# Layer 0's first projection slice by slice, its norm held back, and padded tiles in a two-layer hybrid encoder on one NeuronCore

## The chip, the cores and the metric

The kernel runs on one core of a Trainium2 chip. The core has five engines that run side by side and wait for each other through semaphores: TensorE (PE in the profile, with its weight loads as PEld), VectorE (DVE), ScalarE (ACT), GpSimd (POOL) and SyncE (SP), which here only issues the transfers (DMA) from HBM into SBUF. Matrix products land in PSUM, which has eight banks of 512 float32 columns. The metric is the time of one execution in microseconds on the device, less is better.

## What is computed

A trunk of two layers over 512 tokens of width 1024. Each layer projects the normalised input into queries, keys and values of two groups of heads, runs windowed attention with a sink logit (group A) and differential attention (group B), projects back, and then runs a gated feed-forward part with a depthwise convolution of width 3. Cut to what matters:

```python
for l in range(DEPTH):                                  # 2
    h = rmsnorm(x, g_attn[l])                           # 512 x 1024
    qa, ka, va, qb, kb, vb = split(h @ w_in[l])         # 2304 columns
    qa, ka, qb, kb = (rope(rmsnorm(t, gain)) for t in (qa, ka, qb, kb))
    ya = windowed_gqa_sink(qa, ka, va, sink[l])         # 8 q heads, 2 kv heads
    yb = rmsnorm(diff_attention(qb, kb, vb, lam), subln[l]) * (1 - lambda_init)
    x = x + concat(ya, yb) @ w_out[l]
    h = rmsnorm(x, g_ffn[l])
    gate, val = split(h @ w_up[l])                      # 2 x 2816 columns
    x = x + (silu(conv3(gate)) * val) @ w_down[l]
```

All is float32. The kernel makes each product out of three TensorE products of split operands: high times high, high times low, low times high, where "high" is the value rounded to TensorE's fp32r format and "low" is what the rounding left.

## The kernel before

**Products.** `mm3` (L197) issues the three products of one 128-row slice of the contraction: L198 (high, high), L199 (high, low) and L200 (low, high). The 1024 rows of `x` lie in SBUF as eight tiles `x0` to `x7` of 128 rows by 512 tokens, so a projection is a sum over k = 0..7. In the input projections the stationary operand is a 128-token piece of the normalised input and the moving one a 256-column piece of the weights; in the up-projection (`up`), the down-projection (`dn`) and the first parts of the output projection (`wo`) the weights are stationary and the activations are moving, 512 columns wide.

**Weights.** The weights come as a fixed list of units of at most 512 KB. `emit_unit` (L176) issues one transfer into a tile `wr` (2 buffers), rounds it on ACT into `wh` (L185) and takes the low part on DVE, or on POOL for a part of the units, into `wl` (L186); `wh` and `wl` have 3 buffers each. The first two units, which hold the group A key and value columns of layer 0 (`akv`), are split in four pieces each. `next_unit` keeps three units ahead.

**The norm.** The norm's scale is not put on the input but on the projection's result. `Norm.add` (L212) makes the high part (`na_h`, ACT L216) and the low part (`na_l`, DVE L217) of x times its gain; `Norm.square` squares and sums: in layer 0 the squares of `x0` to `x3` and their sum are made on POOL (L226, L231), those of `x4` to `x7` on ACT (L228) with sums on DVE. `Norm.rms` (L233) sums over the partitions by TensorE products with a column of ones (`na_ss`, L237), and DVE (L240) and POOL (`na_r`, L248, a power of -0.5) turn them into `r_tok`, one factor for each token. Only what reads a projection's bank needs `r_tok`: `scaled` (L330) on ACT.

**The first stage of layer 0.** SP issues `cols`, `x0`, unit 0, `x1` to `x4`, unit 1, `x5` to `x7`, and then the small tables. The projection of `akv` needs two PSUM banks of two 256-column halves, then `aq0` and `aq1` (group A queries, four head columns each) follow; `qk_out` (L336) turns each bank into rotated, normalised and transposed queries or keys, with much of its work on POOL: a power (L248), a product with the rotation table (L362) and a sum (L363). The rest of layer 0's projections are woven with the attention by a planner (`weave`, L125). The order in which instructions stand on each engine is then settled by the scheduler of the tile framework at build time, so it isn't simply the order of the code.

**Places in SBUF.** Tiles are laid out one pool tag behind the other in each partition. As built, the tiles of the tags `wh`, `wl` and `hid0`/`hid1` (the high and low parts of normalised inputs: `na_h`, `na_l`, `nf_h`, `nf_l`) start at bytes 46,144, 58,432, 76,864 and 93,248, multiples of 64. What comes after the tile `rows` (520 numbers, 2,080 bytes) starts 32 bytes above a multiple of 64: `keep` from 129,376, `pair` from 179,168, `prob` from 211,936. `keep` and `pair` hold `act` (the feed-forward's activations, moving operand of `dn`), `yh`/`yl` (moving in `wo`), queries, keys and values; `prob` holds the transposed probabilities (moving in `pv_a` and `yb`). The tag `tmp` has 2,056 bytes and so alternates between the two kinds of start.

Of the kernel before, what the change touches and what calls it, by code (L numbers as in the profile page):

```python
# [16 lines left out]
P = 128  # L17
# [19 lines left out]
FIRST_SQ = 4  # L37
# [5 lines left out]
def kernel(  # L43
# [35 lines left out]
    def tmp(name, n=S):  # L79
        return sb.tile([P, n], F32, tag="tmp", bufs=8, name=name)  # L80
# [61 lines left out]
    cols = const.tile([P, DEPTH, N_COL], F32, name="cols")  # L142
    rope_sb = const.tile([P, 2, NT, HD], F32, name="rope_sb")
    mask_sb = const.tile([P, 3 * P], F32, name="mask_sb")
    ones = const.tile([P, 1], F32, name="ones")
    nhalf = const.tile([P, 1], F32, name="nhalf")
    nc.gpsimd.memset(ones, 1.0)
    nc.gpsimd.memset(nhalf, -0.5)

# [26 lines left out]
    def emit_unit():  # L176
# [7 lines left out]
        for o in ([slice(0, k)] if i > 1 else [slice(j, j + 1) for j in range(k)]):  # L184
            nc.scalar.copy(hi[:, o], raw[:, o])  # L185
            eng.tensor_tensor(out=lo[:, o], in0=raw[:, o], in1=hi[:, o], op=ALU.subtract)  # L186
        ready.append((hi, lo))
        state["emitted"] += 1

# [13 lines left out]
    class Norm:  # L203
        def __init__(self, l, base, name):
            self.l, self.base, self.name = l, base, name
            self.first = l == 0 and base == 0
            self.x = []
            self.hi = [None] * NK
            self.lo = [None] * NK
            self.part = [sb.tile([P, S], F32, tag="tab", bufs=3, name=f"{name}_sum")]  # L210
# [10 lines left out]
        def square(self, k):  # L221
            if self.first and k == FIRST_SQ:
                self.part.append(tmp(f"{self.name}_sum2"))
            sq = self.part[-1] if k == 0 or self.first and k == FIRST_SQ else tmp(f"{self.name}_q{k}")
            if self.first and k < FIRST_SQ:
                nc.gpsimd.tensor_tensor(out=sq, in0=self.x[k], in1=self.x[k], op=ALU.mult)  # L226
            else:
                nc.scalar.activation(sq, self.x[k], AF.Square)  # L228
            if sq is not self.part[-1]:
                eng = nc.vector if self.first and k >= FIRST_SQ else nc.gpsimd  # L230
                eng.tensor_tensor(out=self.part[-1], in0=self.part[-1], in1=sq, op=ALU.add)  # L231

        def rms(self):  # L233
            acc = accum(f"{self.name}_ss")
            for t in range(NT):
                for k, sq in enumerate(self.part):
                    nc.tensor.matmul(acc[:, t:t + 1], lhsT=sq[:, t * P:(t + 1) * P], rhs=ones,  # L237
                                     start=k == 0, stop=k == len(self.part) - 1)
# [11 lines left out]
    def split_out(hi, lo, src):  # L250
        nc.scalar.copy(hi, src)
        nc.vector.tensor_tensor(out=lo, in0=src, in1=hi, op=ALU.subtract)

    warm = const.tile([P, 1], F32, name="warm")
    nc.scalar.activation(warm, ones, AF.Copy, scale=ones)
    nc.sync.dma_start(cols, col_par)
    nc.sync.dma_start(x_sb[0], x_v[:, 0])
    emit_unit()
    for k in range(1, NK):
        nc.sync.dma_start(x_sb[k], x_v[:, k])  # L260
        if k == 4:
            emit_unit()
    nc.sync.dma_start(ident, ident_in)
    nc.sync.dma_start(rope_sb, rope)
    nc.sync.dma_start(mask_sb, mask)
    norm = Norm(0, 0, "na0")
    for k in range(NK):
        norm.add(k, x_sb[k])
# [3 lines left out]
    for l in range(depth):  # L272
        lam_init = 0.8 - 0.6 * math.exp(-0.3 * l)

        rows = sb.tile([P, N_ROW], F32, tag="rows", bufs=1, name=f"rows{l}")
# [33 lines left out]
        r_tok = norm.rms()  # L309
        if l == 0:  # L310
            make_tabs((2, 3))
# [4 lines left out]
        def project(name, done, alloc):  # L316
            w = [next_unit(), next_unit()]
            for tp in range(NT // 2):
                bank = alloc(f"pj{l}_{name}_{tp}").rearrange("p (t c) -> p t c", t=2)
                for i in range(2):  # L320
                    t = 2 * tp + i
                    for k in range(NK):
                        mm3(bank[:, i], (h_in.hi[k][:, t * P:(t + 1) * P], h_in.lo[k][:, t * P:(t + 1) * P]),
# [6 lines left out]
        def scaled(name, bank, tp):  # L330
            raw = rp(name)
            for i in range(2):
                nc.scalar.activation(raw[:, i], bank[:, i], AF.Copy, scale=r_tok[:, 2 * tp + i:2 * tp + i + 1])
# [478 lines left out]
```

## Time and profile before

| | |
|---|---|
| time, median of 3 runs | 1294.73 us (1293.69 to 1295.14) |
| time of the profiled execution | 1294.65 us |
| its span in the profile | 1292.9 us, 17,021 instructions |
| mean granted TensorE clock | 0.977 |
| DVE busy | 754.8 us (58%) |
| ACT busy | 541.8 us (42%) |
| POOL busy | 359.6 us (28%) |
| HBM read, written | 99.73 MB, 2.10 MB |

The profiled execution's time is 1.75 us more than its span. In the profile a row of a timeline gives the start, the duration, the engine, the line, the operation and the names of its output and inputs; several like rows that follow each other are merged with their count. Matrix products overlap in the pipeline, so the time that one costs is the distance between the starts of two neighbours and not its duration.

### The profile page before, as it was taken

To read this page: it belongs to the slowest core of one execution; us is meant where nothing else is said; L and a number is where in the kernel's file an instruction comes from. 1 tells how busy PE (TensorE), PEld (TensorE's weight loads), DVE (VectorE), ACT (ScalarE), POOL (GpSimd) and SP (SyncE) were. 2 spreads that over 40 slices of the span, in tenths; PEclk is the share of its full clock that TensorE was granted. 3 is DMA by queue.
4 is the path that set the end of the run, shared out by engine and by line. 5 is a ranking of instruction groups with operands and counts; after the bars stand their busy time and mean duration, and the time that the engine had idled before them with its cause. 6 is when DMAs were issued, how large, how long until landed. Compare 5 with 4: busy or idle time off the path is not lost. (4 is left out here: it accounts for less than half of the span.)

```text
span 1292.9 us, 17021 instructions
## 1 busy us (share of the span) xinstructions
PE 1239.9 (96%) x6648; PEld 1040.6 (80%) x6648; DVE 754.8 (58%) x1245; ACT 541.8 (42%) x943; POOL 359.6 (28%) x354
## 2 busy tenths in 40 slices
PE   6999997989999999999999999888999999999998
PEld 6988885778888888888899889766888888888886
DVE  6678787766755334554446778756765542355532
ACT  4455564435433213333345666444443331233321
POOL 5746283114111000112247556602321110011100
PEclk8999999899999999999999999969999999999999
DMA  5312121013332333332332111201233323333232
GB/s 174 99 34 66 42 65 34 26 40 103 96 96 87 96 94 114 97 93 72 98 98 81 51 36 64 65 1 34 65 99 113 96 76 98 106 98 98 80 108 90
DMA packets 32625, 102.93 MB, mean 80 GB/s; under 512 B 3616, under 2 KB 4000, under 8 KB 32544
## 3 DMA queue, kind: packets, MB, share of 16 engines
q1 hardware_dynamic: 32544, 101.84, 25.9%
q8 instruction: 52, 0.85, 0.3%
q14 instruction: 29, 0.24, 0.1%
HBM read 99.73 MB, written 2.10 MB: 79 GB/s over the span
## 5 line engine op out<-in xcount | busy, mean ns | idle before, releaser
L185 ACT CAST wh<-wr 128x1024 fp32r<-128x1024 f32 (+3 forms) x210 | 197.5, 944 | 408.6 <-PE up L199 171.0
L199 PE MATMUL up<-nf_l,wh 128*128 128x512 f32 x704 | 274.7, 390 | 0.6 <-DVE nf_l L217 0.5
L200 PE MATMUL up<-nf_h,wl 128*128 128x512 f32 x704 | 274.1, 390 | 0.4
L198 PE MATMUL up<-nf_h,wh 128*128 128x512 f32 x704 | 273.4, 390 | 0.0
L186 DVE TENSOR_TENSOR wl<-wr,wh 128x1024 fp32r<-128x1024 f32 (+3 forms) x174 | 192.5, 1110 | 108.7 <-ACT wh L185 108.4
L718 POOL TENSOR_TENSOR cv<-cv,rb 128x512 f32<-128x512 f32 x44 | 59.2, 1346 | 519.3 <-ACT cv L717 519.3
L199 PEld LDWEIGHTS up<-nf_l,wh 128*128 128x128 f32 x704 | 132.2, 188 | 29.8 <-DVE nf_l L217 2.8
L200 PEld LDWEIGHTS up<-nf_h,wl 128*128 128x128 f32 x704 | 132.2, 188 | 28.8 <-DVE wl L186 1.5
L198 PEld LDWEIGHTS up<-nf_h,wh 128*128 128x128 f32 x704 | 132.2, 188 | 27.5 <-ACT nf_h L216 0.2
L200 PE MATMUL dn<-act,wl 128*128 128x512 f32 x352 | 139.5, 397 | 0.0
L199 PE MATMUL dn<-act,wh 128*128 128x512 f32 x352 | 139.4, 397 | 0.0
L198 PE MATMUL dn<-act,wh 128*128 128x512 f32 x352 | 138.8, 395 | 0.0
L186 POOL TENSOR_TENSOR wl<-wr,wh 128x1024 fp32r<-128x1024 f32 x36 | 86.9, 2419 | 106.4 <-ACT wh L185 106.4
L711 DVE TENSOR_TENSOR gp<-up,rb 128x512 f32<-128x512 f32 x44 | 30.3, 693 | 103.4 <-PE up L200 98.4
L199 PEld LDWEIGHTS dn<-act,wh 128*128 128x128 f32 x352 | 66.8, 190 | 16.5
L198 PEld LDWEIGHTS dn<-act,wh 128*128 128x128 f32 x352 | 66.0, 188 | 16.5
L200 PEld LDWEIGHTS dn<-act,wl 128*128 128x128 f32 x352 | 66.1, 188 | 15.5
L719 DVE TENSOR_TENSOR cv<-cv,up 128x512 f32<-128x512 f32 x44 | 30.2, 687 | 81.8 <-POOL cv L718 72.1
L522 ACT ACTIVATE e_b<-sc_b,mx_b,rqb 128x512 f32<-128x512 f32 x64 | 49.2, 773 | 49.5 <-DVE mx_b L519 45.6
L732 DVE TENSOR_TENSOR x<-x,dn 128x512 f32<-128x512 f32 x32 | 22.0, 689 | 79.7 <-PE dn L200 79.7
L717 ACT ACTIVATE cv<-cv 128x512 f32<-128x512 f32 x44 | 27.7, 631 | 71.6 <-DVE cv L716 71.5
L518 DVE TENSOR_REDUCE mx_b<-sc_b 128x2 f32<-128x1024 f32 x32 | 39.0, 1219 | 7.9 <-PE sc_b L516 7.8
(212 smaller groups left out, 2559.9 us busy)
## 6 DMA issues: line engine op xcount, KB each, us to landing
wr<-w_up SPq DMA_DIRECT2D x88, 512.0 KB, 3.6
wr<-w_in SPq DMA_DIRECT2D x36, 512.0 KB, 3.6
wr<-w_down SPq DMA_DIRECT2D x32, 384.0 KB, 3.0
wr<-w_down SPq DMA_DIRECT2D x32, 320.0 KB, 2.9
wr<-w_out SPq DMA_DIRECT2D x16, 512.0 KB, 3.6
x<-xT SPq DMA_DIRECT2D x8, 256.0 KB, 5.3
outT<-x SPq DMA_DIRECT2D x8, 256.0 KB, 2.0
rows<-row_par SPq DMA_DIRECT2D x2, 260.0 KB, 4.2
```

The costliest lines, as they stand in the source:

```text
L185: nc.scalar.copy(hi[:, o], raw[:, o])
L186: eng.tensor_tensor(out=lo[:, o], in0=raw[:, o], in1=hi[:, o], op=ALU.subtract)
L198: nc.tensor.matmul(acc, lhsT=a[0], rhs=b[0], start=start, stop=False)
L199: nc.tensor.matmul(acc, lhsT=a[0], rhs=b[1], start=False, stop=False)
L200: nc.tensor.matmul(acc, lhsT=a[1], rhs=b[0], start=False, stop=stop)
L518: nc.vector.tensor_reduce(out=mx, in_=scp, axis=AX, op=ALU.max)
L522: nc.scalar.activation(e[c], sc[c], AF.Exp, bias=mx[:, c:c + 1], scale=rq[:, c:c + 1], accum_out=lsum[:, c:c + 1])
L711: nc.vector.tensor_tensor(out=g[:, 1:S + 1], in0=acc[0], in1=rb, op=ALU.mult)
L717: nc.scalar.activation(cv, cv, AF.Silu)
L718: nc.gpsimd.tensor_tensor(out=cv, in0=cv, in1=rb, op=ALU.mult)
L719: nc.vector.tensor_tensor(out=cv, in0=cv, in1=acc[1], op=ALU.mult)
L732: nc.vector.tensor_tensor(out=x_sb[d], in0=x_sb[d], in1=acc, op=ALU.add)
```

## The change

Four things change, all but the last in the first stage of layer 0.

1. **The `akv` projection of layer 0 is run slice by slice.** The first two weight units go to tiles of their own (`first_w`, the raw part in two `prob` buffers), one 128 KB piece of weights is transferred right behind each `x_k`, and for every k the products of all four token tiles are issued into two banks (`mm`) that two products with a column of zeros (L264) have cleared.
2. **The squares are held back and leave POOL.** All eight squares are made on ACT and all seven sums on DVE. They read a scale `gate`, which DVE makes as max and min of an element of the fourth unit's split and which is always 1, so that they can't start before that split is done.
3. **The norm comes later.** One step of `aq0` is issued, then `rms`, then the work on the two `akv` banks between the steps of `aq0`. `aq1`'s first bank is taken from the score tag `sc`.
4. **Tiles are padded.** `tmp` to 528 numbers, `cols` to 112 a layer (its transfer now writes two pieces of 105 numbers to a partition), `rows` to 528; the one-column constants go into one 64-byte tile `unit`. As built, `wh`, `wl`, `hid0` and `hid1` start at 54,336, 66,624, 85,056 and 101,440, each 8,192 bytes above its old place; `keep` starts at 146,048, `pair` at 187,264 and `prob` at 37,952, and every buffer of these tags and of `tmp` starts at a multiple of 64.

```diff
-        eng = nc.gpsimd if kind in ("inb", "out") else nc.vector
-        for o in ([slice(0, k)] if i > 1 else [slice(j, j + 1) for j in range(k)]):
-            nc.scalar.copy(hi[:, o], raw[:, o])
-            eng.tensor_tensor(out=lo[:, o], in0=raw[:, o], in1=hi[:, o], op=ALU.subtract)
+        eng = nc.gpsimd if kind in ("inb", "out") else nc.vector
+        split(eng, hi, lo, raw)
...
         def square(self, k):
-            if self.first and k == FIRST_SQ:
-                self.part.append(tmp(f"{self.name}_sum2"))
...
-            if self.first and k < FIRST_SQ:
-                nc.gpsimd.tensor_tensor(out=sq, in0=self.x[k], in1=self.x[k], op=ALU.mult)
...
+            sq = self.part if k == 0 else tmp(f"{self.name}_q{k}")
+            nc.scalar.activation(sq, self.x[k], AF.Square, **({"scale": gate} if self.first else {}))
+            if k:
+                eng = nc.vector if self.first else nc.gpsimd
+                eng.tensor_tensor(out=self.part, in0=self.part, in1=sq, op=ALU.add)
...
+    for k in range(NK):
+        nc.sync.dma_start(x_sb[k], x_v[:, k])
+        nc.sync.dma_start(first_w[k // 4][0][:, k % 4], units[k // 4][0][:, k % 4])
...
+    for tp in range(2):
+        b = mm(f"pj0_akv_{tp}")
+        nc.tensor.matmul(b, lhsT=zero.broadcast_to([P, P]), rhs=zero.broadcast_to([P, S]), start=True, stop=False)
+        first_banks += [b[:, i * CW:(i + 1) * CW] for i in range(2)]
+    for k in range(NK):
+        norm.add(k, x_sb[k])
+        raw, hi, lo = (v[:, k % 4] for v in first_w[k // 4])
+        split(nc.vector, hi, lo, raw)
+        for t in range(NT):
+            mm3(first_banks[t], (norm.hi[k][:, t * P:(t + 1) * P], norm.lo[k][:, t * P:(t + 1) * P]),
+                (hi, lo), False, k == NK - 1 and t % 2 == 1)
     emit_unit()
...
+    emit_unit()
+    nc.vector.tensor_scalar(out=gate, in0=ready[-1][1][:, 0, :1], scalar1=1.0, scalar2=1.0, op0=ALU.max, op1=ALU.min)
...
-        run(proj_a(0, turn))
-        run(proj_a(1, turn))
+        if l:
+            run(proj_a(0, turn))
+        else:
+            p0 = proj_a(0, at)
+            for _ in range(FIRST_MM):
+                next(p0)
+            r_tok = norm.rms()
+            for tp in range(2):
+                akv_done(first_banks[2 * tp:2 * tp + 2], tp)
+                next(p0)
+            make_tabs((2, 3))
+            run(p0)
+        run(proj_a(1, turn if l else lambda nm: (lambda n: sc2(n)[:, 0], turn)[int(nm[-1])](nm)))
```

On PE the program now starts with the two clearing products and then takes all that needs `x0` before anything that needs `x1` (the numbers behind `na0_h` and `na0_l` are k). Before, its first rows were:

```order
L198 MATMUL pj0_akv_0_233<-wh0_85,na0_h0_119 128x256
L198 MATMUL pj0_akv_1_305<-wh0_85,na0_h0_119 128x256
L199 MATMUL pj0_akv_0_233<-wl0_86,na0_h0_119 128x256
L200 MATMUL pj0_akv_0_233<-wh0_85,na0_l0_120 128x256
L199 MATMUL pj0_akv_1_305<-wl0_86,na0_h0_119 128x256
L200 MATMUL pj0_akv_1_305<-wh0_85,na0_l0_120 128x256
L198 MATMUL pj0_akv_0_233<-wh0_85,na0_h1_123 128x256
```

Of each slice only six products stood there, those of one token tile of each bank; the products of the other two token tiles came after all eight slices, from `x0` again. Now, on PE at the same place:

```order
L264 MATMUL pj0_akv_0_106<-unit_76 128x512
L264 MATMUL pj0_akv_1_108<-unit_76 128x512
L201 MATMUL pj0_akv_0_106<-wh_f0_83,na0_h0_110 128x256
L201 MATMUL pj0_akv_1_108<-wh_f0_83,na0_h0_110 128x256
L202 MATMUL pj0_akv_0_106<-wl_f0_84,na0_h0_110 128x256
L203 MATMUL pj0_akv_0_106<-wh_f0_83,na0_l0_111 128x256
L201 MATMUL pj0_akv_0_106<-wh_f0_83,na0_h0_110 128x256
L202 MATMUL pj0_akv_0_106<-wl_f0_84,na0_h0_110 128x256
L203 MATMUL pj0_akv_0_106<-wh_f0_83,na0_l0_111 128x256
```

The rows of one slice are now twelve, and 96 for the whole projection. The column sums of the squares have moved on PE from between the two halves of `akv` to the end of `aq0`; they now stand after 94 of its 96 products, and `aq1` follows:

```order
L201 MATMUL pj0_aq0_1_470<-wh3_261,na0_h7_236 128x256
L234 MATMUL na0_ss_350<-unit_76,na0_sum_105 128x1 x4
L202 MATMUL pj0_aq0_1_470<-wl3_262,na0_h7_236 128x256
L203 MATMUL pj0_aq0_1_470<-wh3_261,na0_l7_237 128x256
L201 MATMUL pj0_aq1_0_552<-wh4_320,na0_h0_110 128x256
```

On DVE, what stood around the norm of layer 0 before was this (`na0_sum2` is the sum of `x4` to `x7`; `wl2`, `wl3` are the low parts of `aq0`'s weights, `na0_v` the mean square):

```order
L217 SCALAR_TENSOR_TENSOR na0_l7_148<-x7_71,cols_73,na0_h7_147 128x512
L296 TENSOR_SCALAR nsink0_182<-rows0_172 128x8
L300 TENSOR_TENSOR lprod0_184<-rows0_172 128x128
L231 TENSOR_TENSOR na0_sum2_161<-na0_sum2_161,na0_q7_169 128x512
L302 TENSOR_REDUCE ldot0_186<-lprod0_184 128x2
L186 TENSOR_TENSOR wl2_217<-wr2_215,wh2_216 128x1024
L306 TENSOR_SCALAR nlam0_190<-lexp0_188 128x1
L240 TENSOR_SCALAR na0_v_201<-na0_ss_192 128x4
```

Now DVE has, from the end of the slices on, the splits of two units and the gate (L275), behind an instruction that reads `rows`:

```order
L191 TENSOR_TENSOR wl2_256<-wr2_254,wh2_255 128x1024
L191 TENSOR_TENSOR wl3_262<-wr3_260,wh3_261 128x1024
L305 TENSOR_SCALAR nsink0_301<-rows0_291 128x8
L275 TENSOR_SCALAR unit_76<-wl3_262 128x1
L309 TENSOR_TENSOR lprod0_303<-rows0_291 128x128
```

Seven sums and two more splits follow there, and only then the mean square; the last rows of that piece of DVE's program are:

```order
L229 TENSOR_TENSOR na0_sum_105<-na0_sum_105,na0_q7_288 128x512
L191 TENSOR_TENSOR wl4_321<-wr4_319,wh4_320 128x1024
L315 TENSOR_SCALAR nlam0_309<-lexp0_307 128x1
L191 TENSOR_TENSOR wl5_327<-wr5_325,wh5_326 128x1024
L237 TENSOR_SCALAR na0_v_355<-na0_ss_350 128x4
```

`wl3`, `wl4` and `wl5` have moved ahead of the mean square; `wh5`, which `wl5` reads, takes the buffer of `wh2` and so waits on ACT for PE's last product with `wh2`, which is row 84 of `aq0`'s 96. Behind the attention of layer 0 the order of PE, DVE, POOL and ACT is as before.

68 lines of the change are left out of this document (31 added, 37 removed).

## The prediction

> **What bounds the kernel now.** I read the page's busy times first, then its chain, then a table of stretches, then PE's waits.
>
> ```profile
> PE 1239.9 (96%) x6648; PEld 1040.6 (80%) x6648; DVE 754.8 (58%) x1245; ACT 541.8 (42%) x943; POOL 359.6 (28%) x354
> ...
> PE 28%; DVE 0%; issue 0%
> ...
> 0.00:10.00 10.00, 2.77 (x10) 2.32 (x10) 4.62 (x6) 6.55 (x12) 4.75 (x10) 1.00 0.82 279
> 10.00:20.00 10.00, 5.60 (x25) 4.81 (x26) 10.00 (x10) 5.99 (x12) 9.83 (x10) 0.90 0.53 184
> 20.00:30.00 10.00, 10.00 (x68) 10.00 (x68) 4.88 (x11) 0.20 (x1) 1.64 (x4) 0.76 0.31 101
> ...
> 70.00:80.00 10.00, 7.69 (x50) 6.71 (x50) 9.45 (x19) 4.94 (x12) 4.75 (x2) 0.83 0.36 107
> ...
> PE pj_akv L198 <- ACT wh L185: 6.2, 1, 6.2
> PE pj_akv L200 <- DVE na_l L217: 3.8, 2, 2.1
> PE pj_akv L199 <- DVE wl L186: 1.6, 1, 1.6
> PE pt_a L470 <- DVE so_a L454: 2.2, 1, 2.2
> ```
>
> PE works 96% of the span and the chain runs through nothing else that counts, so there are two ways to a shorter time: fewer us in which PE stands or runs at a low clock, and a shorter distance between products. In the stretches (span, busy us by engine PE, PEld, DVE, ACT, POOL, then PE's clock) PE is idle for 7.2 and 4.4 us in the first two, and is granted a clock of 0.76 in the third. The last four lines are PE's waits up to 100 us: the first stage holds 11.6 of them.
>
> **Term 1: when PE gets to `aq0`.** The same projection at two clocks, and the point where `aq0` starts:
>
> ```profile
> 19.65 0.80 PE L200 MATMUL pj_akv<-wh,na_l 128*128 128x256 f32 x2 [1.70 <-DVE na_l L217]
> ...
> 24.30 0.41 PE L198 MATMUL pj_akv<-wh,na_h 128*128 128x256 f32 x1
> 24.51 0.41 PE L199 MATMUL pj_akv<-wl,na_h 128*128 128x256 f32 x1
> ...
> 24.93 0.27 PE L198 MATMUL pj_akv<-wh,na_h 128*128 128x256 f32 x1
> ...
> 31.14 0.28 PE L200 MATMUL pj_akv<-wh,na_l 128*128 128x256 f32 x1
> 31.26 0.28 PE L198 MATMUL pj_aq<-wh,na_h 128*128 128x256 f32 x1
> ```
>
> A product costs 0.21 us up to 24.9 and 0.12 us behind it: full speed comes 5.3 us after work without gaps began at 19.65. The 96 products of `akv` would take 11.5 us at full speed, yet `aq0` starts at 31.26. What feeds them, with the names' lines in ACT, DVE and SP:
>
> ```profile
> 4.53 0.72 ACT L216 ACTIVATE na_h<-x,cols 128x512 fp32r<-128x512 f32 x1 [2.20 <-DMA x<-xT]
> 5.75 1.32 ACT L185 CAST wh<-wr 128x256 fp32r<-128x256 f32 x4 [0.50 <-DMA wr<-w_in]
> 9.23 6.58 DVE L217 SCALAR_TENSOR_TENSOR na_l<-x,cols,na_h 128x512 fp32r<-128x512 f32 x4
> 20.38 0.74 DVE L217 SCALAR_TENSOR_TENSOR na_l<-x,cols,na_h 128x512 fp32r<-128x512 f32 x1
> L186 DVE TENSOR_TENSOR wl<-wr,wh x9: 418/939/1258, 6.2 to 23.4; 128x256 fp32r<-128x256 f32 x8, 128x1024 fp32r<-128x1024 f32 x1
> 11.84 3.42 POOL L231 TENSOR_TENSOR na_sum<-na_sum,na_q 128x512 f32<-128x512 f32 x2
> 2.12 1.85 SPq L260 DMA_DIRECT2D x<-xT  x4
> GB/s 0 0 0 74 194 164 377 258 311 401 336 324 365 365 377 410 434 418 369 406 406 412 378 381 381 386 402 418 336 57 0 0 0 0 0 0 0 0 0 115
> ```
>
> With POOL squaring beside it DVE needs 1.65 us for a `na_l`, and 0.74 alone; a piece of `wl` takes up to 1.26 us, and 0.42 at best. With the squares off POOL a slice costs DVE 0.74 + 0.42 = 1.16 us, ACT 0.72 + 0.33, the transfers 393 KB at about 390 GB/s (the last row, 0 to 20 us) = 1.0, and SP two issues of 0.46. DVE is the slowest: first `wl` at 4.53 + 0.72 + 1.16 = 6.4, the last at 5.25 + 8 x 1.16 = 14.5. PE needs 12 products a slice: 2.56 us at the low clock, 1.44 at the full one, so after the first slice PE is behind its data and has no gaps. If the clock opens 5.3 us later, as it did, at 11.7, 2.1 slices are done and 5.9 x 1.44 = 8.5 remain: `aq0` at 20.2. The bounds: 18.0 if the clock is open at once (6.45 + 8 x 1.44), 21.0 if it takes 7 us, a third longer than the row shows, 27 if it stays low throughout (6.45 + 20.5). The weights of `aq0` follow the slices: two units of 524 KB at 390 GB/s are 2.7 us of transfer, and the second's split ends near 18, in time.
>
> The sum of squares stood ahead of 31.26 and now stands behind; its four columns cost 0.11 each, 0.45. So **term 1 = 31.26 - 20.2 - 0.45 = 10.6 us less** (9.8 to 12.8; 3.8 with the low clock throughout).
>
> What is added here hides. The two clearing products are 512 wide in plain float32; the nearest row below has eight such products 128 wide in 1.09 us, so two take 0.9 us, 1.8 at the low clock, from about 1 to 3 while PE waits for ACT until 5.6; uncovered they would cost 2.3 us only if four times slower. `cols` in 256 pieces lands ahead of `x0`; uncovered 0.4 at most, its own transfer having taken less than 2 us. The gate is one element; the squares with a scale are at worst like `na_h`, 8 x 0.72 from about 18.4, and the sums end near 25 (27 if POOL's tables get in DVE's way), 4 us or more before PE reaches the column sums at 31.5. Behind the gate only the sums and `wl4` wait; `aq1` needs that at 32.
>
> ```profile
> 86.18 1.09 PE L470 MATMUL pt_a<-ident,so_a 128*128 128x128 f32 x8
> ```
>
> **Term 2: the norm's factor and what hangs on it.** It gets later:
>
> ```profile
> 28.48 0.16 DVE L240 TENSOR_SCALAR na_v<-na_ss 128x4 f32<-128x4 f32 x1 [3.76 <-PE na_ss L237]
> 29.90 1.03 POOL L248 TENSOR_TENSOR na_r<-na_v,nhalf 128x4 f32<-128x4 f32 x1
> 35.20 1.19 POOL L248 TENSOR_TENSOR rs_ka<-sv_ka,nhalf 128x4 f32<-128x4 f32 x1 [4.28 <-DVE sv_ka L348]
> 38.72 0.73 POOL L363 TENSOR_TENSOR raw_kv<-raw_kv,sq_ka 128x256 f32<-128x256 f32 x1
> 46.07 1.75 POOL L248 TENSOR_TENSOR rqa<-sv_qa,nhalf 128x8 f32<-128x8 f32 x1 [4.19 <-DVE sv_qa L351]
> 47.79 1.29 POOL L362 TENSOR_TENSOR raw_qa<-raw_qa,tab 128x512 f32<-128x512 f32 x1
> 70.28 4.75 POOL L186 TENSOR_TENSOR wl<-wr,wh 128x1024 fp32r<-128x1024 f32 x2 [2.44 <-ACT wh L185]
> 70.52 5.18 DVE L454 TENSOR_SCALAR so_a<-so_a,rl_a 128x256 f32<-128x256 f32 x4
> ```
>
> Before, it was there at 30.9. Now the mean square waits on DVE behind `wl5`: its buffer is free after 84 products of `aq0` (30.3), its cast and split take 1.05 and 1.23, so 32.6, and POOL's 1.03 gives 33.7, **2.8 us later**, with all four banks of `akv` and `aq0` waiting. Then POOL sets the pace: 2.4 until the first power (my estimate; the rows above have 4.3 from 30.93 to 35.20, but there ACT cast weights in between), two key banks at 1.19 + 2 x 0.73, a table of 1.8, and 4.3 for a query bank (1.75 + 2 x 1.29): the first queries are ready 13.8 us behind the factor, at 47.5. PE has 224 products, 26.9 us, to do from 20.2 until it wants them at 47.1: a wait of 0.4 to 1.0. By the same count the half unit of weights on POOL (2.4) that `bq` needs comes 1.2 late. Against these 2 us stand two losses of before that this order may avoid: PE's wait of 2.2 for `so_a`, which DVE made at 1.3 us each while POOL split weights, and the clock of 0.83 in 70 to 80, worth 1.7. I take **term 2 = 0**, from 4 less (old losses gone, no new ones) to 4 more (both new waits and the 1.9 us of that estimate).
>
> **Term 3: the distance between products in `dn`.** The same stage change, at the full clock, in one timeline, then two far apart rows of `up`, the count, and the other users of the moved tiles:
>
> ```profile
> 483.65 0.40 PE L198 MATMUL dn<-act,wh 128*128 128x512 f32 x1
> 489.98 0.39 PE L198 MATMUL up<-nf_h,wh 128*128 128x512 f32 x1
> 400.03 0.39 PE L198 MATMUL up<-nf_h,wh 128*128 128x512 f32 x1
> 407.51 0.39 PE L198 MATMUL up<-nf_h,wh 128*128 128x512 f32 x1
> L198 PE MATMUL dn<-act,wh 128*128 128x512 f32 x352 | 138.8, 395 | 0.0
> L198 PE MATMUL wo<-yh,wh x32: 392/396/496, 184.1 to 250.2; 128*128 128x512 f32 x32
> L198 PE MATMUL pv_a<-p_a,va x20: 389/394/502, 81.1 to 170.8; 128*128 128x512 f32 x20
> ```
>
> From 483.65 to 489.98 lie 27 products of `dn`: 234.4 ns each. From 400.03 to 407.51 lie 33 of `up`: 226.7. Shape, clock, line and weight tiles are the same; what differs is the tile that streams: `nf_h` and `nf_l` start at a multiple of 64 bytes, `act` 32 above one. `wo` and `pv_a`, which stream from such tiles too, have `dn`'s durations (394 to 396; `up` has 390). The 7.7 ns are also what one more 64-byte piece would cost: a column row of 2,048 bytes has 32 of them, 226.7 / 32 = 7.1. After the padding all these start like `nf_h`, and `nf_h` and the weights stay where they were but for 8,192 bytes. `dn` has 3 x 352 products: 1056 x 7.7 ns = 8.1; I take 7.2 ns, near that piece, 7.6 us. `wo` (288 wide products) and `pv_a` (120) give 2.9 more, half of it hidden in a stage where PE waits anyway: **term 3 = 9.1 less**, 7.6 to 10.5, and 0 if the place isn't the cause; nothing in the rows speaks for a loss beyond 1 us on the 256-wide products. On DVE, ACT and POOL `tmp` already alternates between both starts, and their rows show no second duration.
>
> By the Trainium skill, page "SBUF — State Buffer", section "Specifications (TRN2)", SBUF has lines of 16 bytes; 32 is a multiple of 16, so by that rule an operand 32 bytes off loses nothing, term 3 is 0 and the sum 1284.1. No row here shows 16; the rows fit 64, at 226.7 against 234.4 ns. It is the first rival below. By the page "TensorE: Matmul & The Clock Gate", Part 1, the clock opens after a busy window of about 3.4 us; as an estimate that would be at 9.9 at the earliest and `aq0` at 19.4, the sum 1274.1. The trace's own opening, after 5.3 us, lies within that window and a second one.
>
> **The sum**, against the profiled execution's 1294.65 (0.08 below the median of the runs): 1294.65 - 10.6 + 0 - 9.1 = **1275.0**. Its own range by the bounds is 1267 to 1281.
>
> **The rivals.** *The place in SBUF is not the cause* (the distance between high and low parts, or the region, makes `dn` slower): 1294.65 - 10.6 = 1284. For it: only two tags stream from multiples of 64, so place and stage are mixed. *The factor decides*: POOL's chain behind it has no slack, and PE ends up 2.8 us late instead of 10.6 early, with term 3 intact: 1294.65 + 2.8 - 9.1 = 1288. Against it: POOL idles 4.28 and 4.19 in that chain, since PE fed it. *Slower*: that same chain, without term 3: 1297.5; it decides if PE's lead at the first queries is below 0 and their wait grows past 11 us. *The early start isn't reached*: the clock stays low through all slices: 1294.65 - 3.8 - 9.1 = 1282.
>
> **Chances.** Forecast 0.62, first rival 0.17, factor 0.11, slower 0.06, late start 0.04. The range that leaves out no more than 2 in 10 goes from 1268 to 1288. About 0.2% is what a measurement can tell from no change; faster by more 0.92, within 0.02, slower 0.06.
>
> **What would show it.** Term 1: the first product of `aq0` near 20 in the timeline, `na_l` near 0.74 in the slices, the clock open from about 12. Term 2: `na_r` near 33, waits of PE for POOL between 45 and 60 of 2 us in all. Term 3: `dn` at 227 ns between starts, 390 ns long, and the stretch of layer 1 from 1000 to the end shorter by about 4 us. Wrong would be: `dn` unchanged, or PE waiting more than 5 us for queries behind the factor.

## The result, and the profile after

| | before | changed |
|---|---|---|
| median | 1294.86 us (6 runs, 1293.69 to 1295.26) | 1287.76 us (6 runs, 1287.04 to 1289.58) |
| ratio | | 0.9948, 95% interval 0.9937 to 0.9958 |
| profiled execution, its span | 1294.65, 1292.9 | 1287.35, 1285.6 |

The kernel got faster by 0.5%, 7 us, where 1.5%, 19.7 us, was forecast: inside the range, but little more than a third of the forecast step. Where the rest stayed can be read from the trace stage by stage. First PE, in the changed kernel: the timeline (start, duration) at the clearing products, at the first product of `aq0` and at the first transposes, and then the longest of PE's waits up to 100 us (in all, how many, the longest).

```profile
0.95 3.61 PE L264 MATMUL pj_akv<-unit 128*128 128x512 f32 x4 [0.95 <-POOL unit L149]
...
18.72 0.50 PE L201 MATMUL pj_aq<-wh,na_h 128*128 128x256 f32 x2
...
41.98 0.44 PE L380 MATMUL tr_ka<-ident,raw_kv 128*128 128x128 f32 x2 [0.93 <-DVE raw_kv L374]
...
49.48 0.66 PE L380 MATMUL tr_qa<-ident,raw_qa 128*128 128x128 f32 x4 [0.86 <-POOL raw_qa L372]
```

```profile
PE pt_a L491 <- DVE so_a L475: 4.0, 3, 1.8
PE pj_akv L201 <- ACT wh_f L190: 1.0, 1, 1.0
PE pj_akv L264 <- POOL unit L149: 0.9, 1, 0.9
PE tr_ka L380 <- DVE raw_kv L374: 0.9, 1, 0.9
PE tr_qa L380 <- POOL raw_qa L372: 0.9, 1, 0.9
PE pj_bv L202 <- DVE wl L191: 0.8, 1, 0.8
```

PE starts `aq0` at 18.72 instead of 31.26, 12.5 us earlier; the first wait for `so_a` of before (2.2 us) is not gone but has become three waits of 4.0 us in all. Now the groups of the first score product (`sc_a`) and of `up` in the trace of before (L425, L198) and of the changed kernel (L446, L201); "56.8 to 779.1" are the starts of the first and the last of the group, in layer 0 and layer 1.

```profile
L425 PE MATMUL sc_a<-ka,qah x128: 271/382/447, 56.8 to 779.1; 64*128 64x256 f32 x64, 64*128 64x384 f32 x64
L198 PE MATMUL up<-nf_h,wh x704: 387/389/486, 288.3 to 1232.0; 128*128 128x512 f32 x176
```

```profile
L446 PE MATMUL sc_a<-ka,qah x128: 275/382/579, 53.8 to 775.6; 64*128 64x256 f32 x64, 64*128 64x384 f32 x64
L201 PE MATMUL up<-nf_h,wh x704: 387/389/486, 289.6 to 1226.2; 128*128 128x512 f32 x176
```

Of the 12.5 us, 2.9 are left at the first score, and at the first `up`, where layer 0's feed-forward part begins, the changed kernel is **1.3 us late**. Everything that it wins in the end, it wins behind that point. Set side by side product by product, the lag goes from +1.3 to -1.5 in layer 0's `dn`, to -4.3 in layer 1's attention and to -7.1 in layer 1's `dn`. PE's order is the same from there on, except in layer 1's attention: there, against what is said above under the change, 154 of the 4,919 products stand in another place.

At 127 PE still leads, by 6 to 12 us depending on the product. The next fences show the place where more than half of that goes, 2 to 6 us being left just behind 141: PE, DVE and POOL of the changed kernel, then DVE at the same four multiplications in the kernel before.

```profile
129.51 0.61 PE L446 MATMUL sc_a<-ka,qah 64*128 64x384 f32 x4
...
132.05 0.41 PE L491 MATMUL pt_a<-ident,so_a 128*128 128x128 f32 x2 [1.75 <-DVE so_a L475]
134.70 1.54 PE L491 MATMUL pt_a<-ident,so_a 128*128 128x128 f32 x6 [2.24 <-DVE so_a L475]
...
129.38 5.59 DVE L475 TENSOR_SCALAR so_a<-so_a,rl_a 128x384 f32<-128x384 f32 x4
...
129.17 4.93 POOL L191 TENSOR_TENSOR wl<-wr,wh 128x1024 fp32r<-128x1024 f32 x2 [10.25 <-ACT wh L190]
```

```profile
136.72 1.40 DVE L454 TENSOR_SCALAR so_a<-so_a,rl_a 128x384 f32<-128x384 f32 x4
```

While POOL splits two pieces of weights (129.17 to 134.10), DVE needs 5.59 us for four multiplications that took 1.40 before, when POOL was idle beside them. By the Trainium skill, page "SBUF — State Buffer", section "Who interferes with whom", DVE's `tensor_scalar` can use a pair of ports that it shares with GpSimd, and the one that comes second waits for the other's whole instruction; the trace agrees as to the time, the slowest single multiplication took 2.52 us, about one split of POOL (4.93 / 2). Which ports were used, no row shows. The stretches (span, busy us by PE, PEld, DVE, ACT, POOL, then the granted clock) show what follows:

```profile
115.00:127.00 12.00, 12.00 (x90) 10.66 (x89) 8.27 (x26) 6.68 (x20) 3.84 (x3) 1.00 0.01 1
127.00:134.00 7.00, 3.63 (x28) 2.85 (x26) 6.14 (x9) 4.35 (x10) 4.83 (x2) 1.00 0.19 42
134.00:141.00 7.00, 5.79 (x26) 4.72 (x27) 5.52 (x17) 3.37 (x8) 0.10 (x1) 0.52 0.34 109
```

PE is busy 3.63 of the 7.00 us, and then its clock is halved for 6.8 us: 3.4 us of standing in the one stretch, 1.2 in the other, and 3.4 lost to the clock. In the kernel before, 127 to 141 had no gap and the full clock:

```profile
127.00:141.00 14.00, 14.00 (x111) 12.79 (x110) 11.43 (x33) 8.01 (x20) 5.63 (x5) 1.00 0.11 37
```

It is one place of several. Over the whole way from the first product of `aq0` to the first `up`, in the kernel before and then in the changed one:

```profile
31.26:288.30 257.04, 236.58 (x1618) 204.44 (x1617) 187.31 (x393) 132.44 (x293) 117.38 (x83) 0.96 0.17 51
```

```profile
18.72:289.60 270.88, 240.38 (x1625) 207.34 (x1625) 201.72 (x407) 140.18 (x303) 124.84 (x93) 0.94 0.17 51
```

PE stands for 30.5 us instead of 20.5 (270.88 - 240.38, 257.04 - 236.58), and by the records of its clock runs at half clock for 30.7 us instead of 20.5, which costs another 5.1. That is 15.1 us on a way that is 13.8 us longer.

Last, `dn`, from one product to the first `up` behind it, 79 products on:

```profile
471.61 0.39 PE L203 MATMUL dn<-act,wl 128*128 128x512 f32 x1
...
489.69 0.40 PE L201 MATMUL up<-nf_h,wh 128*128 128x512 f32 x1
```

18.08 us for 79 products are 228.9 ns each, where it had been 234.4; `up` has kept its 226.9.

### The profile page after: what moved, and what is told of

Read it like the earlier page. It is cut to its first block, busy times and chain, and to the rows that moved or that the text cites. A ratio compares the mean times of both kernels' runs of the same rounds, so it can differ in the third digit from the quotient of the medians.

```text
span 1285.6 us, 17039 instructions
## 1 busy us (share of the span) xinstructions
PE 1232.1 (96%) x6644; PEld 1035.6 (81%) x6644; DVE 756.1 (59%) x1250; ACT 546.7 (43%) x947; POOL 350.9 (27%) x348
## 5 line engine op out<-in xcount | busy, mean ns | idle before, releaser
L190 ACT CAST wh<-wr 128x1024 fp32r<-128x1024 f32 (+2 forms) x202 | 195.0, 966 | 405.4 <-PE up L202 171.1
L201 PE MATMUL up<-nf_h,wh 128*128 128x512 f32 x704 | 273.5, 390 | 0.0
L191 DVE TENSOR_TENSOR wl<-wr,wh 128x1024 fp32r<-128x1024 f32 (+2 forms) x166 | 185.5, 1118 | 107.3 <-ACT wh L190 107.0
L201 PEld LDWEIGHTS up<-nf_h,wh 128*128 128x128 f32 x704 | 132.1, 188 | 27.4 <-ACT nf_h L219 0.2
L201 PE MATMUL dn<-act,wh 128*128 128x512 f32 x352 | 138.4, 394 | 0.0
L202 PE MATMUL dn<-act,wh 128*128 128x512 f32 x352 | 136.3, 388 | 0.0
L201 PEld LDWEIGHTS dn<-act,wh 128*128 128x128 f32 x352 | 66.2, 188 | 13.2
L475 DVE TENSOR_SCALAR so_a<-so_a,rl_a 128x256 f32<-128x256 f32 (+1 forms) x64 | 47.1, 794 | 0.0
```

The costliest lines, as they stand in the source:

```text
L190: nc.scalar.copy(hi, raw)
L191: eng.tensor_tensor(out=lo, in0=raw, in1=hi, op=ALU.subtract)
L201: nc.tensor.matmul(acc, lhsT=a[0], rhs=b[0], start=start, stop=False)
L202: nc.tensor.matmul(acc, lhsT=a[0], rhs=b[1], start=False, stop=False)
L475: nc.vector.tensor_scalar(out=so[i][:, :n], in0=so[i][:, :n], scalar1=rl[:, i:i + 1], scalar2=None, op0=ALU.mult)
```

## The experiments

Two things had to be separated: the padding from the new first stage, and, within layer 0, the causes that could take PE's lead. Times are medians; each ratio is to runs of the kernel before on the same chip. "Left out" marks a kernel that doesn't compute everything. First score and first `up` come from one trace per kernel, whose time differs from the median by up to 2 us; half-clock stretches of 3.4 us, each worth 1.7, come and go in these traces, so a difference below some 3 us tells little there.

| kernel | first score | first `up` | median | ratio (95%) |
|---|---|---|---|---|
| before | 56.8 | 288.3 | 1294.86 | |
| changed | 53.8 | 289.6 | 1287.76 | 0.9948 (0.9937 to 0.9958) |
| `pad_only` | 56.1 | 289.3 | 1291.64 | 0.9974 (0.9964 to 0.9984) |
| `no_pad` | 54.1 | 292.0 | 1294.03 | 0.9995 (0.9980 to 1.0010) |
| `keep16` | 53.6 | 291.3 | 1291.69 | 0.9988 (0.9975 to 1.0001) |
| `no_split` (left out) | 52.6 | 267.3 | 1268.51 | 0.9810 (0.9779 to 0.9840) |
| `before_no_split` (left out) | 56.1 | 274.9 | 1281.02 | 0.9892 (0.9878 to 0.9907) |
| `early_factor` (left out) | 46.8 | 280.4 | 1280.30 | 0.9887 (0.9866 to 0.9909) |
| `early_keep` (other factor) | 48.4 | 284.7 | 1283.13 | 0.9912 (0.9897 to 0.9927) |
| `dve_split` | 53.4 | 284.8 | 1286.04 | 0.9932 (0.9915 to 0.9948) |
| `ungated` | 48.4 | 282.8 | 1279.72 | 0.9889 (0.9867 to 0.9911) |
| `rms_first` | 48.6 | 282.6 | 1279.91 | 0.9898 (0.9883 to 0.9914) |
| `ungated_dve` | 49.0 | 274.3 | 1272.27 | 0.9839 (0.9822 to 0.9857) |
| `rms_first_dve` | 50.0 | 277.0 | 1273.29 | 0.9842 (0.9827 to 0.9858) |

### The padding alone, and the new stage alone

`pad_only` is the kernel before with this edit; `no_pad` is the changed kernel with the opposite one.

```diff
-        return sb.tile([P, n], F32, tag="tmp", bufs=8, name=name)
+        return sb.tile([P, S + 16], F32, tag="tmp", bufs=8, name=name)[:, :n]
...
-        rows = sb.tile([P, N_ROW], F32, tag="rows", bufs=1, name=f"rows{l}")
+        rows = sb.tile([P, N_ROW + 8], F32, tag="rows", bufs=1, name=f"rows{l}")[:, :N_ROW]
```

> The kernel before with only `rows` and `tmp` padded; the order of instructions on every engine is that of before, and `keep`, `pair` and `prob` now start at multiples of 64 bytes. Theory A (the start of the moving tile costs `dn` some 5 ns a product, and the first stage's change is worth nothing in the end): `dn` goes from 234 to 229 ns between starts, layer 1's stage behind 1000 loses 2.7 us, and the time is 1294.8 - 8.6 = 1286 (1285 to 1289), no slower than the changed kernel. Rival B (`dn` got shorter for another reason, a new place of the tile in the partition or the new order): `dn` stays at 234 and the time at 1294 to 1295.

> The changed kernel with `rows` and `tmp` as before the change; the order of instructions is that of the changed kernel, `keep` and `pair` start 32 bytes above a multiple of 64, `prob` stays on one. Theory A: `dn` back at 234 ns, first `up` at 289 to 291 as in the changed kernel, and the time 1287.8 + 5.6 (`dn`) + up to 3 (`wo` and layer 1) = 1293.4 to 1296.4: the new first stage alone gains nothing. Rival C (the early start is worth its 10 us and something in the padding gives it back in layer 0's attention): first `up` near 280, time 1290 or less.

`dn` in the timeline of `pad_only`, 78 products from the first row to the second:

```profile
471.74 0.39 PE L198 MATMUL dn<-act,wh 128*128 128x512 f32 x1
...
489.68 0.40 PE L198 MATMUL up<-nf_h,wh 128*128 128x512 f32 x1
```

17.94 / 78 = 230.0 ns: rival B falls, the places do it, with every engine's order as before. In `no_pad` `dn` needs 233.3 (mean of its 1052 distances), and its first `up` comes at 292.0, so rival C falls too: without the padding the early start isn't worth anything. Theory A's price was too high: `pad_only` gains 0.26% and not 0.7%, since `dn` brings 4.5 us and layer 1's attention 0.3 of the 3 put down for `wo` and the rest, while the first `up` comes 0.9 us later than in the kernel before. The two halves give 0.31% of the 0.52%; the 0.21% between them is about what the intervals of the three ratios leave open. In the traces, `dn` is 1.1 ns slower in `pad_only` than in the changed kernel, whose `act` lies elsewhere, and layer 1's attention is 2.8 us shorter in the changed kernel than before, against 0.3 in `pad_only` and 1.9 in `no_pad`.

That stage goes by the clock. From the last `dn` of layer 0 to the first `up` of layer 1 it takes 262.8 to 263.7 us in the traces where PE is at half clock for 30.7 us of it, 260.9 to 262.1 where it is for 27.3, 259.9 to 260.6 for 23.9 and 258.6 for 20.5. The kernel before has 30.7, the changed one 27.3; but `early_factor`, `early_keep` and `dve_split` below, which have the padding and the slices too, have 30.7 and 263.3 to 263.5 us, as before. So these 2.8 us can't be put down to the change, and what sets the number of such stretches is open.

### 16 bytes instead of 64

```diff
-        return sb.tile([P, 2, S], F32R, tag="keep", bufs=10, name=name)
+        return sb.tile([P, 2 * S + 16], F32R, tag="keep", bufs=10, name=name)[:, 4:4 + 2 * S].rearrange("p (a s) -> p a s", a=2)
```

> The changed kernel with all ten buffers of `keep` moved to 16 bytes above a multiple of 64, `pair` left on one; the order of instructions is that of the changed kernel. `act` lies in both, so one run compares them. If the start against 64 bytes is what counts, `dn` products that stream from `keep` go from 229 to 233 or 234 ns between starts and those from `pair` stay at 229: 2 to 3 us more in all. If only a start that isn't a multiple of 16 or 32 costs, or if the region does, both stay at 229 and the time is that of the changed kernel. By the Trainium skill, page "SBUF — State Buffer", section "Specifications (TRN2)", lines are 16 bytes, which speaks for the second.

The timeline of `keep16`, with 81 products of `dn` between the rows:

```profile
473.64 0.40 PE L201 MATMUL dn<-act,wh 128*128 128x512 f32 x1
...
492.50 0.40 PE L201 MATMUL up<-nf_h,wh 128*128 128x512 f32 x1
```

18.86 / 81 = 232.8 ns, 3.9 more than in the changed kernel, 4.1 us over 1,056 products; by the ratios the time is 0.40% more, 5.2 us. So a start at a multiple of 16 isn't enough, against the prediction's first rival in the form that a multiple of 16 bytes loses nothing. But the products from `pair`, which had stayed on multiples of 64, became as slow as those from `keep` (232.8 and 232.6 on average). `act` alternates between the two, slice by slice, so either the stream as a whole is set by its tiles together, or `pair`'s own move (640 bytes up) did it. A simple rule of 64 bytes for each product is refuted; what the rule is stays open.

### POOL's splits

In `no_split` and `before_no_split` the low parts of the 18 weight units of layer 0 that POOL makes are left out, in the changed kernel and in the kernel before.

```diff
-        split(eng, hi, lo, raw)
+        if i < 26 and eng is nc.gpsimd:
+            nc.scalar.copy(hi, raw)
+            lo = hi
+        else:
+            split(eng, hi, lo, raw)
```

> The changed kernel without the low parts of the 18 weight units that POOL splits in layer 0 (their low part is the high part again; the products stay). Theory D (PE's lead of 10.3 us at 127 is lost to collisions of POOL's splits with DVE's multiplication of `so_a`, 5.59 instead of 1.4 us at 129, and to the half clock behind them): the four multiplications take 1.4 us everywhere, the lead lasts, first `up` at 279 to 284, time 1278 to 1283. Rival E (the chain of the softmaxes, which starts with the first queries, sets the pace, and its lead is only 4 to 5 us at best): PE waits in other places instead, first `up` at 287 to 290, time 1285 to 1288.

> The kernel before, with the low parts of the same 18 weight units of layer 0 left out (their low part is the high part again; the products stay); not padded. The control for `no_split`, whose first `up` came at 267.3. If the early start is worth its 10 us once POOL's splits are out of the way, first `up` here stands at 276 to 280. If the splits alone set the pace and the early start is worth nothing even then, it stands at 266 to 270, as in `no_split`.

The first `up` of `no_split`, then of `before_no_split`:

```profile
L205 PE MATMUL up<-nf_h,wh x704: 387/389/486, 267.3 to 1205.7; 128*128 128x512 f32 x176
```

```profile
L198 PE MATMUL up<-nf_h,wh x704: 387/389/486, 274.9 to 1217.0; 128*128 128x512 f32 x176
```

Without the splits the first `up` comes 13.4 us earlier in the order of before and 22.3 in the changed one. Both had paid for them, far more than either theory had expected, and the changed kernel 9 us more. (The 32 multiplications of layer 0 keep DVE busy for 21.6 us before, 28.6 in the changed kernel and 10.2 in `before_no_split`.) With them gone, the early start is worth 7.6 us at the first `up`: neither all nor nothing. Leaving the work out also takes it off POOL's own chain and changes the order on PE in layer 0; `dve_split` changes the order too, but keeps the work and moves it to DVE.

```diff
-        eng = nc.gpsimd if kind in ("inb", "out") else nc.vector
+        eng = nc.gpsimd if kind in ("inb", "out") and i >= 26 else nc.vector
```

> The changed kernel, result kept: the 18 weight units of layer 0 that POOL split are split on DVE, at about 1.2 instead of 2.4 us each, which adds some 22 us to DVE between 45 and 250. Theory D (POOL's splits slow DVE's `so_a` and by that PE): the four multiplications take 1.0 to 1.5 us everywhere, first `up` 285 or less, time 1283 or less. Rival G (DVE has no room in the softmax chain): first `up` 289 or later, time 1287 or more.

The group of the 32 multiplications of layer 0 (shortest, median and longest in ns) in the changed kernel and in `dve_split`:

```profile
L475 DVE TENSOR_SCALAR so_a<-so_a,rl_a x32: 339/414/2521, 66.8 to 161.7; 128x256 f32<-128x256 f32 x16, 128x384 f32<-128x384 f32 x16
```

```profile
L475 DVE TENSOR_SCALAR so_a<-so_a,rl_a x32: 344/378/421, 68.8 to 153.8; 128x256 f32<-128x256 f32 x16, 128x384 f32<-128x384 f32 x16
```

No multiplication is longer than 421 ns now, and the first `up` comes 4.8 us earlier, at 284.8, though DVE has 18 splits more: theory D, of the collisions, holds in that part. The time misses its 1283 by 3 us; by the ratios it is 0.16% below the changed kernel's, which isn't clear of noise, while the same step taken from `ungated`, below, is. PE now waits elsewhere, mostly for the softmax of group B, which has DVE in it (up to the first `up`; in the changed kernel these four are 5.3, 4.5, 0 and 0, with 9.8 for `so_a`, which is gone here):

```profile
PE sc_b L537 <- ACT e_b L543: 9.0, 5, 3.3
PE wt_b L563 <- DVE e_b L551: 4.9, 2, 4.0
PE sc_a L446 <- DVE mx_a L450: 3.1, 2, 2.9
PE pv_a L201 <- DVE yl L191: 2.5, 1, 2.5
```

### The factor

`early_factor` makes the factor from the squares of `x0` alone and leaves out the other seven squares and the sums. `early_keep` makes it from the same squares, but makes all the held-back work as well and doesn't use it.

```diff
-            nc.scalar.activation(sq, self.x[k], AF.Square, **({"scale": gate} if self.first else {}))
+            nc.scalar.activation(sq, self.x[k], AF.Square, **({"scale": ones} if self.first else {}))
...
+    norm.square(0)
...
-    for k in range(NK):
-        norm.square(k)
```

> The changed kernel with layer 0's first norm factor made from the squares of `x0` alone, not held back: seven squares and seven sums are left out, and `na_r` is there near 10 us and not at 34.9. Theory E (the chain from the factor to the first queries sets the pace): first `sc_a` moves from 53.8 to 45 or less, and first `up` from 289.6 to 284 or less, time 1282 or less. Theory D (collisions behind 127): first `sc_a` moves as well, but first `up` stays within 2 us of 289.6, time 1286 to 1290. Rival F (the factor is late by little and PE has other work meanwhile): neither moves by more than 2 us.

```diff
+            self.src = self.part
...
-                nc.tensor.matmul(acc[:, t:t + 1], lhsT=self.part[:, t * P:(t + 1) * P], rhs=ones,
+                nc.tensor.matmul(acc[:, t:t + 1], lhsT=self.src[:, t * P:(t + 1) * P], rhs=ones,
...
+    norm.src = sb.tile([P, 4, CW], F32, tag='prob', bufs=4, name='na0_src').rearrange('p a b -> p (a b)')[:, :S]
+    nc.scalar.activation(norm.src, x_sb[0], AF.Square)
```

> The changed kernel with the factor of layer 0's first norm made early from the squares of `x0` alone, as in `early_factor`, but with all eight held-back squares and seven sums still made (and not used). The control for `early_factor`: if the early factor made its gain, first `up` at 279 to 282 and time 1279 to 1282; if the work left out of ACT and DVE made it, first `up` at 287 to 290 and time 1285 to 1288.

The power (`na_r`) came at 24.1 and 23.8, not near 10 as expected: POOL makes the rotation tables ahead of it, and the row data that these need land at 18 and 19. Even so the first `up` moves by 9.2 us in `early_factor` and by 4.9 in `early_keep`, the first score by 7.0 and 5.4, the time by 0.61% and 0.36%. So half of it or more is the factor's own time, and the rest the held-back work itself: in `early_keep` ACT squares from 20.6 to 25.6 and casts a unit behind that, so that it reads out the first `akv` bank at 26.5, though the factor is there at 25.2; DVE sums from 21.9 to 27.6, and POOL waits until 27.6 with a table that takes the sum's buffer. Theory E, that the chain from the factor sets the pace, holds as to its direction; rival F falls, and theory D by itself too. E's numbers were too bold: the first score came at 46.8, not 45.

`ungated` is the same question with the result kept; the squares read a constant one and may run as `x` arrives.

```diff
-            nc.scalar.activation(sq, self.x[k], AF.Square, **({"scale": gate} if self.first else {}))
+            nc.scalar.activation(sq, self.x[k], AF.Square, **({"scale": ones} if self.first else {}))
```

> The changed kernel, result kept: the squares of layer 0's first norm read a constant one and not the gate, so they aren't held back; the column sums now stand on PE 8 products ahead of the end of `akv`. Theory E (what the early start is worth hangs on the factor): `na_r` near 22 to 25 and not 34.9, first `sc_a` at 50 or less, `aq0` 1 to 3 us later than 18.7, since DVE then has 1.84 us a slice; first `up` at 281 to 285, time 1279 to 1283. Rival (holding the squares back is what makes the early start possible): `aq0` at 24 or later, first `up` at 288 or later, time 1286 or more.

The first score and `up` of `ungated`, and POOL around the factor:

```profile
L446 PE MATMUL sc_a<-ka,qah x128: 277/381/444, 48.4 to 768.8; 64*128 64x256 f32 x64, 64*128 64x384 f32 x64
L201 PE MATMUL up<-nf_h,wh x704: 387/389/486, 282.8 to 1217.2; 128*128 128x512 f32 x176
...
20.05 2.83 POOL L296 TENSOR_TENSOR tab<-rope_sb,rows 128x128 f32<-128x128 f32 x2
...
25.08 0.89 POOL L296 TENSOR_TENSOR tab<-rope_sb,rows 128x128 f32<-128x128 f32 x2
25.91 1.03 POOL L245 TENSOR_TENSOR na_r<-na_v,unit 128x4 f32<-128x4 f32 x1
```

As theory E has it: the factor 8 us earlier, the first score 5.4, the first `up` 6.8, and the time 8 us below that of the changed kernel (0.59% by the ratios). PE's last product of `akv` comes at 20.80 instead of 18.52, and 0.8 of that are the column sums, which now stand ahead of it; so holding the squares back isn't what makes the early start possible, and is worth 1.5 us there.

`rms_first` was to bring the factor earlier still, by writing its instructions ahead of the tables.

```diff
+    r_tok = norm.rms()
     for l in range(depth):
...
-            r_tok = norm.rms()
```

> As `ungated`, result kept, with the factor's instructions ahead of the rotation tables and of the first step of `aq0` in the program. In `ungated` the column sums end at 19.5, but the mean square comes at 22.5 behind two splits on DVE and the power at 25.9 behind 6.7 us of tables on POOL. If the factor still decides, `na_r` comes at 20 to 22, first `sc_a` moves from 48.4 to 44 to 47, and first `up` from 282.8 to 279 to 281. If by now PE has its work ahead and the chain has room, first `sc_a` may move but first `up` stays within 1 us.

The scheduler left the tables ahead, `na_r` came at 26.2 instead of 25.9, and nothing else moved. That says nothing about the factor.

### Both causes taken away

`ungated_dve` has the edits of `ungated` and `dve_split`, and `rms_first_dve` that of `rms_first` too.

> The changed kernel, result kept, with the squares not held back (as `ungated`) and the 18 weight units of layer 0 split on DVE instead of POOL (as `dve_split`). If the late factor and POOL's splits are two separate losses, the gains add: first `up` at 282.8 - 4.9 = 278 (276 to 280), time 1275 (1273 to 1277). If they are one loss, first `up` stays at 281 to 284 and the time at 1279 to 1281.

> `rms_first` with the 18 weight units of layer 0 split on DVE, result kept. If all three losses are separate, first `up` comes at 274 to 277 and the time is 1271 to 1275; if DVE becomes the bound, it is not below that of `ungated_dve`.

```profile
L201 PE MATMUL up<-nf_h,wh x704: 388/389/487, 274.3 to 1210.6; 128*128 128x512 f32 x176
```

Against the first `up` of the changed kernel at 289.6, not holding back is worth 6.8 us, DVE's splits 4.8, and both 15.3: two losses that add, 3.7 us more than their sum and outside the 276 to 280 that had been expected, on the better side. By the ratios they are 0.59%, 0.16% and 1.09%; the 0.34% beyond the sum is about what the four intervals leave open. Taken from `ungated`, moving the splits to DVE is worth 8.5 us at the first `up` and 0.50% of the time, which is clear. At 274.3 the first `up` is 14.0 us ahead of that of the kernel before; but no run moved the splits in the kernel before, so how much of that is the early start isn't shown. `ungated_dve` is the fastest kernel here that keeps the result: 1272.27 us, ratio 0.9839 (0.9822 to 0.9857), faster than both kernels of this case. `rms_first_dve` can't be told from it.

## Why the prediction was wrong

**Term 1 (PE at `aq0`) was right**, and too small: 31.26 - 18.72 - 0.45 = 12.1 us against 10.6. PE had almost no gap in the slices, as forecast (waits of 0.33 and 0.14 us), and DVE made a `na_l` in 0.75 us (0.74 forecast). Most of the 1.5 us are the clock; with a clock open from the start the prediction's own bound was 18.0, 2.2 earlier than its 20.2. The prediction let it open at 11.7, 5.3 us behind the first real product; its row for that, at 24.9 in the kernel before, was a second opening, since products follow each other at 0.12 there from 16.95 on already, and the clock stands at full from 14.7 to 18.1. In the changed kernel's trace the first record of the granted clock, at full, begins at 4.3, and from 6.6 on most products follow each other at 0.12 us. The clearing products keep PE busy from 0.95 on, four records of 3.61 us in all where 0.9 to 1.8 had been put down; they hide, as was said, and probably open the clock early, but no run took them away. In the ten other kernels here with the early start that first record begins between 3.9 and 10.6, and `aq0` between 18.2 and 19.7; with the old order the record begins between 14.7 and 23.3. By the Trainium skill, page "TensorE: Matmul & The Clock Gate", Part 1, the clock is judged in windows of about 3.4 us that run freely; the trace agrees, the half-clock stretches of these traces are 3.4 us or a multiple where the end doesn't cut them.

**Term 2 was the failing step**: "I take term 2 = 0, from 4 less (old losses gone, no new ones) to 4 more". At the first `up` the changed kernel is 1.3 us late where term 1 alone would have it 12.1 early: 13.4 us came back. The parts of the step, against the runs:

- The factor was put at 33.7 and came at 34.9. Its 1.02 us of POOL stand behind 1.7 us of tables, which the sum had not counted.
- The first queries were put at 47.5, and their transposes start at 49.48; from 40 to 51 PE waits 2.6 us, for keys, queries and a split of weights (0.9, 0.9, 0.8), against 2 forecast. So far the count was nearly right.
- "PE has 224 products, 26.9 us, to do from 20.2 until it wants them at 47.1", and so hardly a loss: this treated PE as the engine that sets the end from the first queries on. The table of the experiments shows otherwise. In the kernels where POOL splits, the first `up` comes 231 to 238 us behind the first score, whenever PE had begun `aq0`: 231.5 in the kernel before, 235.8 in the changed one, 234.4 in `ungated`. So what counts there is mainly when the queries are ready, and the change moved the first score by 3.0 us only, and then took 4.3 longer from there. PE's lead was real, but it was a stock of other work done ahead, and it was used up in 10.0 us more of waits, those for `so_a` ahead of all, and 5.1 lost to the clock. Where POOL doesn't split, the stretch is shorter: 214.7 and 218.8 without the splits, 225.3 to 231.4 with them on DVE.
- "Two losses of before that this order may avoid": the wait for `so_a` and the clock behind it. They were not avoided. They come from POOL's splits standing beside DVE's multiplications (5.18 us for four in the prediction's own row, 5.59 at 129 now), and a PE that is early only waits longer there: it arrives at the same `so_a` with its other work already done. The prediction had the row and named the split beside it, but took it for a loss that another order may avoid, not for a cost that all orders here with POOL's splits pay somewhere: the longest multiplication of layer 0 lasts 2.52 to 2.64 us in each of them.

**Term 3 (the places) was right in sign and too large**: 9.1 forecast, 6.5 found in the products. `dn` went from 234.4 to 229.0 ns and not to 227, which is 1056 x 5.4 = 5.7 us against 7.6. `wo` went from 233.0 to 230.3, 0.8 us; `pv_a`, 233.2 before and 234.6 now, gained nothing. `pad_only` shows the effect by itself, and with it falls the first rival, that the place is not the cause; `keep16` shows that the mechanism put forward, one more piece of 64 bytes for each product, is at best incomplete.

**The rivals.** "The factor decides" had a chance of 0.11 and 1288, and the time was 1287.8. That the factor's chain sets the pace `early_keep` and `ungated` confirm; the rest of this rival didn't happen. It had no slack in that chain and PE late at once by 2.8, while in fact the first score followed the factor by 18.9 us instead of 25.9 and came 3.0 earlier, the lead lasted to 127, and POOL's splits took a part of it too. That the times agree is luck: a first `up` 1.3 us late instead of 2.8, 6.5 for term 3 instead of 9.1, and 2.8 us of layer 1's attention that were in no sum. The slower rival, the same without term 3, is nearly `no_pad`: 1294.0 measured, 1297.5 forecast.

The sum in the changed kernel's trace, by stages: +1.3 to the first `up`, -2.8 in layer 0's `dn`, -2.8 in layer 1's attention, -2.8 in layer 1's `dn`: -7.1 of the -7.3 us between the two profiled executions.

## What to carry to other kernels

When PE is 96% busy, a head start of PE is still worth only what it brings forward of the chain that PE waits for later: find the first point where PE needs another engine's result, and ask how much earlier that result comes. Work held back "behind" a critical start has to come before the next result that counts, or it takes the gain back (here a gate of one element cost some 8 us). And that GpSimd is busy only 28% of the time doesn't make work on it free: look for DVE instructions that last several times their shortest duration, and see what GpSimd does beside them.

## What the runs showed of the hardware

- 512-wide fp32r products at the full clock follow each other at 226.9 ns in `up`, and in `dn` at 229.0 to 234.4, depending on where the tiles of `act` lie: `dn` has 234.4 and 233.3 with `act` 32 bytes above a multiple of 64 in two regions, 230.1 and 229.0 on a multiple in two, and 232.7 when half its tiles lie 16 bytes above one. What sets these steps is not settled.
- The DVE multiplication `so_a` lasts 0.34 to 0.42 us with no split beside it and up to 2.6 us beside a weight split of POOL; without 18 such splits layer 0's first `up` comes 13 and 22 us earlier in the two orders, although POOL is busy 28 and 27% of the span.
